# A trunk layer with mixing steps taken one group later and the merges' operand loads in another order

## The chip, the cores and the metric

The kernel runs on one core of a Trainium2 chip. The metric is the device time of one execution in microseconds (us). A core has TensorE (PE; its weight loads are listed as PEld), VectorE (DVE), ScalarE (ACT), GpSimd (POOL) and SyncE (SP). Every transfer of this kernel that the profile lists is issued from SP's queue. Each engine takes its own list of instructions in a fixed order; an instruction whose inputs or buffers aren't ready holds up all that stand behind it on that engine.

## The reference: what is computed

One layer of a decoder trunk for 1024 tokens and 16 leading meta tokens, 2048 wide, in float32. The layer normalizes the rows, makes one wide input projection, and runs two branches on it: stick-breaking attention and causal pooling over four window lengths. Each branch is gated, projected up to 2048 columns, gated again and summed; an output projection, a residual sum and a final normalization follow. The parts that matter here:

```python
zin = h @ w_in
q, k, v, g_attn, u, g_pool, m_attn, m_pool = jnp.split(zin, cuts, axis=-1)
o_attn = stick_breaking_attention(q, k, v) * silu(g_attn)
y_attn = o_attn @ w_attn_up
pooled = multiscale_pool(u)          # per group g: mean over the last 2, 4, 8 or 16 tokens, minus the token
mixed = einsum('blgc,gcd->blgd', pooled, pool_w)      # four groups of 256 channels
o_pool = mixed * pool_scale * silu(g_pool)
y_pool = o_pool @ w_pool_up
merged = sigmoid(m_attn) * y_attn + sigmoid(m_pool) * y_pool
return x + merged @ w_out
```

## The kernel before

All products are made in three parts: an operand is split into an upper part (a copy rounded to the matmul's format, ScalarE, line 116) and a lower part (the difference, VectorE or GpSimd, line 117), and `mm3` (line 137) adds upper x upper, upper x lower and lower x upper in PSUM. So each loaded tile of 128 x 512 costs one transfer of 256 KB, one ScalarE copy and one subtraction before TensorE can use it.

The input projection is done for pairs of 128-column blocks, called duos, with seven products for a two by two block matrix. A first stage makes four of them per duo and leaves partial sums in device memory (`d_nu`, `d_up`, `d_c`). A second stage, `duo_steps` (line 584), makes the three others per duo in three passes `m5`, `n4`, `p3`: each pass loads its weights in two quarters (`wr`), splits them (`wh`, `wl`), multiplies, and VectorE evicts the accumulators together with a partial sum (lines 592 and 594). The third pass goes on in the accumulators of the first.

The stages in the profiled execution: the first stage of the projection, whose last partial sums are stored at 977 us; three duos of the gates of the pooling branch (`gp`) and then, up to about 1169 us, the four pooling groups; attention, with the remaining duos between its steps, to 1876 us; the merges, from 1907 to 2270 us; the output projection to the end.

*A pooling group* (lines 675 to 714) before the change is, in program order: load and split the group's 256 x 256 mixing weights (`pwh`, `pwl`, one buffer each); load the first quarter of its `u`; run the duo, which fills `us[0]` and `us[1]`; for each of the two halves of channels build window sums by doubling (line 692: one addition for window 2, four for window 16), then the mean minus the token (line 697), then split it into `ph` and `pl`; then the mixing step: four accumulators of 128 x 512, six matmuls each, evicted by VectorE with the scale and the gate (line 713) into one of two buffers `st` and stored to `d_op`. In the last group the duo of the last gate stands between the split and the mixing step.

*The merges* (from line 897) multiply the gated branch outputs by `w_pool_up` (blocks of kind "p") and `w_attn_up` (kind "a"). One block makes 128 output columns for both halves of the tokens, `t` = 0 and 1, 24 matmuls each, and takes two weight tiles. The operands stay on chip: `op[t]` from `d_op` and `oa[t]` from `d_oa`, eight tiles for each half. `fill` (line 899) loads one of them through one of six buffers `ol` and splits it. The table `order` (line 926) begins with three "p" blocks, 0, 8 and 1, and then takes "a" blocks between. Before the loop come the two gate tiles of the first block and `op[0]` and `op[1]`; the first block's weights are issued after the sixth load of `op[0]` (`issue_after`, line 910; the `[5]` in line 906); `oa[0]` and `oa[1]` are filled ahead of the first and second block. Between the blocks GpSimd makes linear forms of blocks of `w_out` (`w_forms`, line 183), with four loads `cw` and four stores `d_wf` per round.

The building framework turns this program into one list per engine, and in doing so may move instructions that don't depend on each other. The rows of these lists are shown with the change.

Of the kernel before, what the change touches and what calls it, by code (L numbers as in the profile page):

```python
# [9 lines left out]
F32 = mybir.dt.float32  # L10
# [62 lines left out]
def trunk_kernel(  # L73
# [154 lines left out]
    with ExitStack() as actx:  # L228
# [408 lines left out]
        with ExitStack() as a0ctx:  # L637
# [36 lines left out]

            for g, win in enumerate(WINDOWS):
                pwh = a0.tile([P, 512], F32R, tag="pwh", name=nm("pwh"), bufs=1)
                pwl = a0.tile([P, 512], F32R, tag="pwl", name=nm("pwl"), bufs=1)
                load_split(pwh, pwl, pool_w[g].rearrange("(c p) d -> p c d", p=P))
                pwh, pwl = (t.rearrange("p (c d) -> p c d", d=256) for t in (pwh, pwl))
# [4 lines left out]
                duo(d, lambda key: half_of(us[key[0]], key[1], META), lambda key, t: None, us[1][:, :META])  # L684
                ph, pl = [None] * 2, [None] * 2
# [14 lines left out]
                if g == GROUPS - 1:  # L700
                    sils.append(sil_tiles())
                    silu_duo(a0, named["gp", g], sils[g])
                sil = sils[g]
                for dc in range(2):
                    dd = slice(dc * P, (dc + 1) * P)
                    ch = 2 * g + dc
                    for i in range(2):
                        t = slice(i * 512, (i + 1) * 512)
                        a = acc_tile()
                        for n, cc in enumerate((1, 0)):  # L710
                            mm3(a, pwh[:, cc, dd], pwl[:, cc, dd], ph[cc][:, t], pl[cc][:, t], n == 0, n == 1)
                        st = a0.tile([P, 512], F32, tag="st", name=nm("st"), bufs=2)
                        nc.vector.scalar_tensor_tensor(out=st, in0=a, scalar=psc[:, ch : ch + 1], in1=sil[dc][:, t], op0=ALU.mult, op1=ALU.mult)
                        nc.sync.dma_start(d_op[ch][:, t], st)
# [182 lines left out]
    with tc.tile_pool(name="pm", bufs=2, side="right", reuse_waits="tile") as pm:  # L897

        def fill(A, j, src):
            raw = pm.tile([P, 512], F32, tag="ol", name=nm("ol"), bufs=6)  # L900
            ins = nc.sync.dma_start(raw, src)
            put(A, j, raw)
            return ins
# [48 lines left out]
        for n, (kind, c) in enumerate(order):  # L952
            if n in (0, 1):
                fill_up(oa[n], d_oa, n)
# [231 lines left out]
```

## Time and profile before

| | |
|---|---|
| median of 3 runs | 2588.54 us (2584.05 to 2588.91) |
| the profiled execution's own time | 2589.82 us |
| its span, first to last instruction | 2588.1 us |
| mean granted clock of TensorE | 0.982 |
| busy share: PE, DVE, ACT, POOL | 95%, 49%, 35%, 39% |
| transfers | 457.81 MB, mean 177 GB/s |

The profile is one execution. Its page gives busy times by engine, the span in 40 slices, and the groups of instructions; the other views (waits, timelines by engine, stretches of time) are answers from the same trace. In a row such as `L713 ... st<-acc,psc,sl` the number is the line of the kernel, and out<-in are the program's names. What stands in brackets at the end of a timeline row is the idle time of the engine before the instruction and what ended it. A matmul's stated duration overlaps its neighbours; the distance from start to start is what it costs.

### The profile page before, as it was taken

The page shows a single profiled execution, that of the slowest core. Times are in us where ns is not written, and L with a number is a line of the kernel's source. Part 1 is how long each engine was busy: PE and PEld are TensorE (multiplying, and loading weights), DVE is VectorE, ACT ScalarE, POOL GpSimd, SP SyncE. Part 2 cuts the span into 40 slices and gives each one's busy share as a digit, 9 for nine tenths or more (in the row PEclk, how much of TensorE's full clock was granted, in tenths as well). Part 3 has the DMA queues.
Part 4 walks back from the last instruction along what each step waited for, and adds up shares of the span by engine and source line. Part 5 has one row for each costly group of instructions (what it writes and reads, how often), then busy time and mean ns, then how long its engine had stood idle before and what let it go on. Part 6 is the DMA issues. An engine that isn't in the chain of part 4 may idle for free.

```text
span 2588.1 us, 35874 instructions
## 1 busy us (share of the span) xinstructions
PE 2462.5 (95%) x12680; PEld 2087.6 (81%) x12680; DVE 1268.1 (49%) x2089; ACT 896.8 (35%) x1845; POOL 1005.4 (39%) x898
## 2 busy tenths in 40 slices
PE   6899999999999999899999999999949999989998
PEld 5676778888888887888888888888748888867887
DVE  5442234553333344575676567656652322445556
ACT  6421122222222234224454455545431111144243
POOL 1655555554454544233323333333104545520212
PEclk8999999999999999999999999999979999999999
DMA  5566555665555557435334443443286777675534
GB/s 181 168 208 212 196 195 201 215 232 175 179 184 183 184 179 231 133 115 151 123 118 136 127 126 117 141 126 91 86 280 208 250 237 246 225 248 183 190 124 171
DMA packets 390516, 457.81 MB, mean 177 GB/s; under 512 B 32432, under 2 KB 234544, under 8 KB 389296
## 3 DMA queue, kind: packets, MB, share of 16 engines
q1 hardware_dynamic: 390336, 455.53, 54.7%
q8 instruction: 99, 1.62, 0.3%
q14 instruction: 81, 0.66, 0.1%
HBM read 313.11 MB, written 142.31 MB: 176 GB/s over the span
## 4 chain that ended last, share of the span: by engine, by line
PE 77%; DMA 7%; DVE 6%; POOL 3%; ACT 2%; issue 2%; SPq 0%; DVEq 0%; POOLq 0%; ACTq 0%
PE acc L138 17%; PE acc L140 17%; PE acc L139 17%; PE accb L138 4%; PE accb L139 4%; PE accb L140 4%; POOL r L270 3%; PE accb L1012 2%; PE accb L1011 2%; PE accb L1010 2%; DMA mr<-d_f 2%; DMA raw<-in_w_in_dram 2%; PE tr L764 1%; DVE s L692 1%; DVE x L117 1%
## 5 line engine op out<-in xcount | busy, mean ns | idle before, releaser
L138 PE MATMUL acc<-x,wh 128*128 128x512 f32 (+2 forms) x2736 | 980.1, 359 | 25.2 <-ACT wh L116 16.4
L140 PE MATMUL acc<-x,wl 128*128 128x512 f32 (+2 forms) x2736 | 971.1, 355 | 7.3 <-DVE wl L117 6.0
L139 PE MATMUL acc<-x,wh 128*128 128x512 f32 (+2 forms) x2736 | 968.8, 354 | 0.0
L138 PEld LDWEIGHTS acc<-x,wh 128*128 128x128 f32 x2736 | 519.4, 190 | 97.0 <-ACT wh L116 22.1
L140 PEld LDWEIGHTS acc<-x,wl 128*128 128x128 f32 x2736 | 518.3, 189 | 85.3 <-DVE wl L117 13.3
L139 PEld LDWEIGHTS acc<-x,wh 128*128 128x128 f32 x2736 | 519.4, 190 | 62.7
L116 ACT ACTIVATE wh<-wr 128x512 fp32r<-128x512 f32 x408 | 256.6, 630 | 593.7 <-PE accb L139 235.4
L117 DVE TENSOR_TENSOR wl<-wr,wh 128x512 fp32r<-128x512 f32 x288 | 221.1, 770 | 248.2 <-ACT wh L116 230.0
L117 DVE TENSOR_TENSOR wl<-r,wh 128x512 fp32r<-128x512 f32 x160 | 149.5, 938 | 345.6 <-ACT wh L116 328.5
L117 POOL TENSOR_TENSOR wl<-wr,wh 128x512 fp32r<-128x512 f32 x120 | 166.6, 1388 | 346.0 <-ACT wh L116 289.3
L116 ACT ACTIVATE wh<-r 128x512 fp32r<-128x512 f32 x160 | 100.3, 631 | 474.9 <-POOL r L270 369.6
L270 POOL TENSOR_TENSOR r<-raw,raw 128x512 f32<-128x512 f32 x80 | 111.1, 1388 | 379.2 <-DMA raw<-in_w_in_dram 348.9
L138 PE MATMUL accb<-x,wh 128*128 128x512 f32 x512 | 200.2, 391 | 32.4 <-ACT wh L116 32.4
L270 POOL TENSOR_TENSOR r<-r,raw 128x512 f32<-128x512 f32 x160 | 221.6, 1385 | 12.5 <-DMA raw<-in_w_in_dram 2.5
L139 PE MATMUL accb<-x,wh 128*128 128x512 f32 x512 | 199.9, 390 | 0.0
L140 PE MATMUL accb<-x,wl 128*128 128x512 f32 x512 | 199.7, 390 | 0.0
L1010 PE MATMUL accb<-wh,x 128*128 128x512 f32 x416 | 163.8, 394 | 7.1 <-ACT wh L116 7.0
L1012 PE MATMUL accb<-wl,x 128*128 128x512 f32 x416 | 164.2, 395 | 0.2
L1011 PE MATMUL accb<-wh,x 128*128 128x512 f32 x416 | 162.7, 391 | 0.0
L748 DVE TENSOR_TENSOR_SCAN wt<-wt 128x272 f32<-128x272 f32 (+5 forms) x128 | 107.7, 842 | 110.2 <-POOL wt L743 64.8
L117 DVE TENSOR_TENSOR wl<-raw,wh 128x512 fp32r<-128x512 f32 x136 | 102.6, 765 | 100.9 <-ACT wh L116 100.8
L116 ACT ACTIVATE wh<-raw 128x512 fp32r<-128x512 f32 x160 | 97.6, 624 | 135.2 <-PE acc L139 100.3
(176 smaller groups left out, 3059.5 us busy)
## 6 DMA issues: line engine op xcount, KB each, us to landing
raw<-in_w_in_dram SPq DMA_DIRECT2D x96, 512.0 KB, 5.8
d_r<-r SPq DMA_DIRECT2D x160, 256.0 KB, 2.0
wr<-d_r SPq DMA_DIRECT2D x160, 256.0 KB, 2.9
raw<-in_w_in_dram SPq DMA_DIRECT2D x152, 256.0 KB, 5.3
wr<-in_w_in_dram SPq DMA_DIRECT2D x80, 256.0 KB, 3.0
cw<-in_w_out_dram SPq DMA_DIRECT2D x64, 256.0 KB, 5.1
d_wf<-cw SPq DMA_DIRECT2D x64, 256.0 KB, 2.8
wr<-d_wf SPq DMA_DIRECT2D x64, 256.0 KB, 3.0
```

Source lines behind the costliest of these rows:

```text
L116: nc.scalar.activation(hi, src, AF.Copy)
L117: (eng or nc.vector).tensor_tensor(out=lo, in0=src, in1=hi.bitcast(F32), op=ALU.subtract)
L138: nc.tensor.matmul(ps, wh, rh, start=first, stop=False, skip_group_check=skip)
L139: nc.tensor.matmul(ps, wh, rl, start=False, stop=False, skip_group_check=skip)
L140: nc.tensor.matmul(ps, wl, rh, start=False, stop=last, skip_group_check=skip)
L270: nc.gpsimd.tensor_tensor(out=t, in0=a, in1=b, op=ALU.add)
L692: nc.vector.tensor_tensor(out=nxt[:, lo:], in0=cur[:, lo:], in1=cur[:, lo - sh : TOK - sh], op=ALU.add)
L748: nc.vector.tensor_tensor_scan(out=rev, data0=rev, data1=rev, initial=wt[:, w : w + 1], op0=ALU.mult, op1=ALU.bypass)
L764: nc.tensor.transpose(tr[:, n, :], bt[:, off : off + P], ident)
L1010: nc.tensor.matmul(a, sh, wh, start=first and j == 0, stop=False, skip_group_check=not first)
L1011: nc.tensor.matmul(a, sl, wh, start=False, stop=False, skip_group_check=not first)
L1012: nc.tensor.matmul(a, sh, wl, start=False, stop=j == KH - 1, skip_group_check=not first)
```

## The change

Two parts. In the pooling groups the mixing step of group g is put behind the duo of group g + 1; its weights (now `pw0`, `pw1`, loaded by `mix_weights`) are loaded ahead of that duo. The last group's mixing step stays behind the last gate duo. Within a mixing step the order of the matmuls is unchanged in the program: half 1 first, half 0 second, for each accumulator.

In the merges the six buffers `ol` move to a pool of their own, `po`, opened ahead of `pm`. Program order becomes: `op[0]`; the gates of block 0; its weights, issued after the first load of `op[0]` at the earliest (`[0]`); then, between the two halves of block 0, `op[1]`; then `oa[0]` ahead of the second block and `oa[1]` ahead of the third.

```diff
@@ -672,16 +672,37 @@
                 for calls in every:
                     calls[i]()
 
+            mixed = {}
+
+            def mix_weights(g):
+                pw = [a0.tile([P, 512], F32R, tag=f"pw{m}", name=nm("pw"), bufs=1) for m in range(2)]
+                load_split(*pw, pool_w[g].rearrange("(c p) d -> p c d", p=P))
+                return [t.rearrange("p (c d) -> p c d", d=256) for t in pw]
+
+            def mix(g, pwh, pwl):
+                ph, pl = mixed.pop(g)
+                for dc in range(2):
+                    dd = slice(dc * P, (dc + 1) * P)
+                    ch = 2 * g + dc
+                    for i in range(2):
+                        t = slice(i * 512, (i + 1) * 512)
+                        a = acc_tile()
+                        for n, cc in enumerate((1, 0)):
+                            mm3(a, pwh[:, cc, dd], pwl[:, cc, dd], ph[cc][:, t], pl[cc][:, t], n == 0, n == 1)
+                        st = a0.tile([P, 512], F32, tag="st", name=nm("st"), bufs=2)
+                        nc.vector.scalar_tensor_tensor(out=st, in0=a, scalar=psc[:, ch : ch + 1], in1=sils[g][dc][:, t], op0=ALU.mult, op1=ALU.mult)
+                        nc.sync.dma_start(d_op[ch][:, t], st)
+
             for g, win in enumerate(WINDOWS):
-                pwh = a0.tile([P, 512], F32R, tag="pwh", name=nm("pwh"), bufs=1)
-                pwl = a0.tile([P, 512], F32R, tag="pwl", name=nm("pwl"), bufs=1)
-                load_split(pwh, pwl, pool_w[g].rearrange("(c p) d -> p c d", p=P))
-                pwh, pwl = (t.rearrange("p (c d) -> p c d", d=256) for t in (pwh, pwl))
+                if g:
+                    pw = mix_weights(g - 1)
                 d = named["u", g]
                 us = [tok_tile(a0, "u", F32) for _ in range(2)]
                 nc.sync.dma_start(us[0][:, META : META + HALF], d_c[d.n])
                 nc.sync.dma_start(us[0][:, :META], d_cm[d.n])
                 duo(d, lambda key: half_of(us[key[0]], key[1], META), lambda key, t: None, us[1][:, :META])
+                if g:
+                    mix(g - 1, *pw)
                 ph, pl = [None] * 2, [None] * 2
                 for cc in (1, 0):
                     u = us[cc]
@@ -697,21 +718,11 @@
                     nc.vector.scalar_tensor_tensor(out=raw, in0=cur[:, META:], scalar=1.0 / win, in1=u[:, META:], op0=ALU.mult, op1=ALU.subtract)
                     split(pool_h, pool_l, raw)
                     ph[cc], pl[cc] = pool_h, pool_l
-                if g == GROUPS - 1:
-                    sils.append(sil_tiles())
-                    silu_duo(a0, named["gp", g], sils[g])
-                sil = sils[g]
-                for dc in range(2):
-                    dd = slice(dc * P, (dc + 1) * P)
-                    ch = 2 * g + dc
-                    for i in range(2):
-                        t = slice(i * 512, (i + 1) * 512)
-                        a = acc_tile()
-                        for n, cc in enumerate((1, 0)):
-                            mm3(a, pwh[:, cc, dd], pwl[:, cc, dd], ph[cc][:, t], pl[cc][:, t], n == 0, n == 1)
-                        st = a0.tile([P, 512], F32, tag="st", name=nm("st"), bufs=2)
-                        nc.vector.scalar_tensor_tensor(out=st, in0=a, scalar=psc[:, ch : ch + 1], in1=sil[dc][:, t], op0=ALU.mult, op1=ALU.mult)
-                        nc.sync.dma_start(d_op[ch][:, t], st)
+                mixed[g] = ph, pl
+            pw = mix_weights(GROUPS - 1)
+            sils.append(sil_tiles())
+            silu_duo(a0, named["gp", GROUPS - 1], sils[-1])
+            mix(GROUPS - 1, *pw)
 
         with tc.tile_pool(name="a1", bufs=1, side="right", reuse_waits="tile") as a1:
             MK = 64 + META
@@ -894,16 +905,18 @@
         q, jj = divmod(j, QD)
         split(A[q][0][:, jj], A[q][1][:, jj], src)
 
-    with tc.tile_pool(name="pm", bufs=2, side="right", reuse_waits="tile") as pm:
+    with ExitStack() as mctx:
+        po = mctx.enter_context(tc.tile_pool(name="po", bufs=6, side="right", reuse_waits="tile"))
+        pm = mctx.enter_context(tc.tile_pool(name="pm", bufs=2, side="right", reuse_waits="tile"))
 
         def fill(A, j, src):
-            raw = pm.tile([P, 512], F32, tag="ol", name=nm("ol"), bufs=6)
+            raw = po.tile([P, 512], F32, tag="ol", name=nm("ol"))
             ins = nc.sync.dma_start(raw, src)
             put(A, j, raw)
             return ins
 
         def fill_up(A, d_o, t):
-            return [fill(A, j, d_o[j][:, t * HALF : (t + 1) * HALF]) for j in range(KH)][5]
+            return [fill(A, j, d_o[j][:, t * HALF : (t + 1) * HALF]) for j in range(KH)][0]
 
         def up_mm(w, o, c, behind):
 
@@ -927,9 +940,13 @@
         for n, k in enumerate((("p", 0), ("p", KH), ("p", 1))):
             order.remove(k)
             order.insert(n, k)
-        first = [gate("sp", 6, d_sp, 0, t) for t in range(2)]
-        op, oa = [xquads(0, HALF, xo), xquads(1, HALF, xo)], [xquads(2, HALF), xquads(3, HALF, xc)]
-        behind = [fill_up(op[t], d_op, t) for t in range(2)][0]
+        op, oa = [], []
+
+        def more(into, d_o, t, *where):
+            into.append(xquads(*where))
+            return fill_up(into[t], d_o, t)
+
+        behind = more(op, d_op, 0, 0, HALF, xo)
         sps, ms = {}, {}
 
         def sums(j):
@@ -950,12 +967,14 @@
 
         forms = w_forms(pm)
         for n, (kind, c) in enumerate(order):
-            if n in (0, 1):
-                fill_up(oa[n], d_oa, n)
+            if n in (1, 2):
+                more(oa, d_oa, n - 1, *((2, HALF), (3, HALF, xc))[n - 1])
             if kind == "p":
-                gs = [gate("sp", 6, d_sp, c, t) for t in range(2)] if n else first
+                gs = [gate("sp", 6, d_sp, c, t) for t in range(2)]
                 for t, a in up_mm(w_pu, op, c, None if n else behind):
                     nc.vector.tensor_tensor(out=gs[t], in0=a, in1=gs[t], op=ALU.mult)
+                    if n + t == 0:
+                        more(op, d_op, 1, 1, HALF, xo)
                 sps[c] = gs
             else:
                 gs = [gate("sa", 6, d_sa, c, t) for t in range(2)]
```

What the lists of the engines become at three places. First SP at the start of the merges. Before (`sp` are gate tiles, `ol` operand loads, `wr` weights, `cw` blocks of `w_out`):

```order
L923 DMA sp_18844<-d_sp_104 128x512
L901 DMA ol_18862<-d_op_80 128x512
...
L901 DMA ol_18922<-d_op_87 128x512
L901 DMA ol_18926<-d_oa_72 128x512
...
L901 DMA ol_18954<-d_oa_79 128x512
L124 DMA wr_18960<-in_w_pool_up_dram 128x4x128
L124 DMA wr_18966<-in_w_pool_up_dram 128x4x128
L189 DMA cw_19022<-in_w_out_dram 128x512
```

Between the rows shown are 14 further loads from `d_op` and six from `d_oa`: 24 operand loads stand ahead of the first weights. With the change:

```order
L850 DMA d_sp_118<-st_18766 128x512
L914 DMA ol_18849<-d_op_80 128x512
...
L914 DMA ol_18877<-d_op_87 128x512
L936 DMA sp_18881<-d_sp_104 128x512
L936 DMA sp_18883<-d_sp_104 128x512
L124 DMA wr_18887<-in_w_pool_up_dram 128x4x128
L124 DMA wr_18893<-in_w_pool_up_dram 128x4x128
L914 DMA ol_18927<-d_op_80 128x512
...
L914 DMA ol_18955<-d_op_87 128x512
L189 DMA cw_18985<-in_w_out_dram 128x512
```

Eight operand loads stand ahead of the first weights. Behind the last row come three more `cw`, the eight loads of `oa[0]`, two gates, and then the weights of the second block; behind these four stores `d_wf`, the eight loads of `oa[1]`, two gates and the weights of the third block.

Second, VectorE in the first merge block, with the change (`x<-ol` is the lower part of an operand, `sp<-accb` the eviction of one half of a block):

```order
L117 TENSOR_TENSOR x_3646_18926<-ol_18955,x_3645_18925 128x512
L975 TENSOR_TENSOR sp_18881<-accb_18897,sp_18881 128x512
L117 TENSOR_TENSOR x_3661_18994<-ol_18997,x_3660_18993 128x512
L117 TENSOR_TENSOR x_3661_18994<-ol_19001,x_3660_18993 128x512
L117 TENSOR_TENSOR x_3661_18994<-ol_19005,x_3660_18993 128x512
L975 TENSOR_TENSOR sp_18883<-accb_18959,sp_18883 128x512
L117 TENSOR_TENSOR x_3661_18994<-ol_19009,x_3660_18993 128x512
```

Before, 28 operand parts and the two weight parts stood ahead of the first eviction; now the lower parts of `oa[0]` stand behind the eviction of the first half, and those from the fourth on behind that of the second.

Third, VectorE around the mixing step of group 1 before (`s` are window sums, `st<-acc` the mixing evictions):

```order
L697 SCALAR_TENSOR_TENSOR s_9671<-s_9671,u_9459 128x1024
L117 TENSOR_TENSOR pl_9673<-s_9671,ph_9674 128x1024
L713 SCALAR_TENSOR_TENSOR st_9685<-acc_9678,psc,sl_8660 128x512
L713 SCALAR_TENSOR_TENSOR st_9695<-acc_9688,psc,sl_8660 128x512
L117 TENSOR_TENSOR pwl_9719<-wr_9720,pwh_9718 128x512
```

and, with the change, around the mixing step of group 0, which now stands at this place:

```order
L592 TENSOR_TENSOR u_9413<-nu_9419,acc_9422 128x256
L713 TENSOR_TENSOR s_9663<-u_9413 128x1039
L693 SCALAR_TENSOR_TENSOR st_9621<-acc_9614,psc,sl_8658 128x512
L693 SCALAR_TENSOR_TENSOR st_9631<-acc_9624,psc,sl_8658 128x512
L693 SCALAR_TENSOR_TENSOR st_9641<-acc_9634,psc,sl_8659 128x512
L117 TENSOR_TENSOR pl_9658<-s_9656,ph_9659 128x1024
L693 SCALAR_TENSOR_TENSOR st_9651<-acc_9644,psc,sl_8659 128x512
L713 TENSOR_TENSOR s_9665<-s_9663 128x1037
L117 TENSOR_TENSOR pw_9673<-wr_9674,pw_9672 128x512
```

The mixing evictions stood behind the chain of their own group; they now stand among the window sums of the next.

## The prediction

> **What bounds the kernel now.** I read the page first, then the waits of TensorE, then the two stages that the change touches, engine by engine.
>
> ```profile
> PE 2462.5 (95%) x12680; PEld 2087.6 (81%) x12680; DVE 1268.1 (49%) x2089; ACT 896.8 (35%) x1845; POOL 1005.4 (39%) x898
> PEclk8999999999999999999999999999979999999999
> ```
>
> TensorE is busy for 95% of the span; only stages in which it stands still, or runs at a lower granted clock, can give time. One slice of the clock row falls to 7, at about 1880 us, the start of the merges. The waits around it, and those of TensorE alone from 1000 to 1180 us (the pooling groups):
>
> ```profile
> PE accb L138 <- ACT wh L116: 32.4, 2, 31.1
> ...
> PE acc L138 <- ACT ph L116: 11.1, 5, 3.7
> PE acc L138 <- ACT wh L116: 1.9, 1, 1.9
> PE acc L139 <- DVE pl L117: 1.5, 3, 0.7
> ```
>
> One wait of 31.1 us opens the merges; eight waits of up to 3.7 us, for the split halves ph and pl of the pooled channels, stand before the mixing steps. A stretch of each kind in the windows view (columns: stretch, length, busy time of PE, PEld, DVE, ACT, POOL, granted clock, DMA share, GB/s):
>
> ```profile
> 1061.20:1064.60 3.40, 3.40 (x24) 3.17 (x23) 2.52 (x5) 0.63 (x1) 0.00 (x0) 0.94 0.42 154
> 1112.70:1116.10 3.40, 3.08 (x7) 1.97 (x8) 3.37 (x3) 0.00 (x0) 0.00 (x0) 0.52 0.74 229
> 1880.80:1907.50 26.70, 0.00 (x0) 0.00 (x0) 15.94 (x24) 15.56 (x25) 0.00 (x0) 0.50 0.92 289
> 1907.50:1911.40 3.90, 3.84 (x9) 3.02 (x10) 1.39 (x2) 0.82 (x3) 1.56 (x2) 0.50 1.03 368
> 2000.00:2100.00 100.00, 100.00 (x442) 82.78 (x442) 28.34 (x36) 11.39 (x18) 55.47 (x41) 1.00 0.71 233
> ```
>
> After each gap TensorE first runs at half clock: nine products in 3.9 us at 1907.5, where 442 in 100 us is one per 0.226 us, so a restart costs about 1.8 us more than its gap. While TensorE stands, the transfers work at 0.92 share and 289 GB/s: the wait is one for data. From 2000 us TensorE is full; what is won before passes to the end.
>
> **The mixing steps.** Each group of channels is a duo of three passes, the window sums on VectorE, and 24 mixing products. VectorE's timeline, first eviction of the first pass of each group (and of the second pass, second row), then the chain that group 2 waits for:
>
> ```profile
> 1040.45 0.42 DVE L594 TENSOR_TENSOR u<-acc,up 128x256 f32<-128x256 f32 x1 [1.27 <-PE acc L140]
> 1046.32 0.42 DVE L594 TENSOR_TENSOR u<-acc,up 128x256 f32<-128x256 f32 x1 [1.27 <-PE acc L140]
> ...
> 1068.01 0.42 DVE L594 TENSOR_TENSOR u<-acc,up 128x256 f32<-128x256 f32 x1 [1.27 <-PE acc L140]
> ...
> 1098.23 0.42 DVE L594 TENSOR_TENSOR u<-acc,up 128x256 f32<-128x256 f32 x1 [1.28 <-PE acc L140]
> ...
> 1117.46 1.23 DVE L697 SCALAR_TENSOR_TENSOR s<-s,u 128x1024 f32<-128x1024 f32 x1
> 1119.81 1.22 DVE L117 TENSOR_TENSOR pl<-s,ph 128x1024 fp32r<-128x1024 f32 x1 [1.12 <-ACT ph L116]
> ...
> 1125.69 0.75 DVE L713 SCALAR_TENSOR_TENSOR st<-acc,psc,sl 128x512 f32<-128x512 f32 x1 [0.19 <-DMA d_op<-st]
> ...
> 1129.86 0.42 DVE L594 TENSOR_TENSOR u<-acc,up 128x256 f32<-128x256 f32 x1 [1.28 <-PE acc L140]
> ```
>
> The groups take 27.56, 30.22 and 31.63 us. Their own work: a pass takes 5.87 us (1040.45 to 1046.32), the third has 256 columns for a mean of 264 and takes 5.69, the mixing 24 x 0.226 = 5.42; together 5.87 + 5.87 + 5.69 + 5.42 = 22.85 us. The excess is 4.7 + 7.4 + 8.8 = 20.9 us, and with the pl wait of 0.7 before the last mixing 21.6. That is idle time and half clock together. The excess grows with the window because one more VectorE addition (about 1.2 us) stands in each half's chain per doubling.
>
> Moved behind the next duo, a mixing step needs ph and pl some 17 us later; the chain of 5 to 10 us lies under the three passes. What VectorE has to do per group: for window 8 two halves of three additions, mean and lower part, 5 x 1.23 each, 12.3; evictions 6 x 0.42 + 0.2 = 2.7; mixing evictions 4 x 0.75 = 3.0; lower parts of weights 4 x 0.7 = 2.8: 20.8 us, under 22.85. Window 16 adds 2.5, 23.3, but its chain has mixing step 2 and the gate duo (three passes of 24 products, 16.3 us) in front of its own mixing. In VectorE's queue the mixing evictions now stand among the chain of the next group, and they wait for TensorE and for the store two before; what is behind them and urgent is the eviction of the next first pass, needed 5.87 us after it is ready, when the third pass accumulates on the same accumulator. The step's transfers move on SP's queue too:
>
> ```profile
> d_op<-st SPq DMA_DIRECT2D x16, 256.0 KB, 2.4
> ...
> wr<-in_pool_w_dram SPq DMA_DIRECT2D x4, 256.0 KB, 3.0
> ```
>
> Four stores per step, 2.4 us each from two buffers, with products every 1.36 us (6 x 0.226): the third eviction waits about 1 us, on VectorE, which has it to spare. The weights pw keep one of the four wr buffers until the mixing before is done; three are left for six weight loads in 22.85 us, each held for about 3.0 + 0.6 + 1.4 = 5 us: one per 1.7 us against one per 2.9 needed. I leave 0.35 us per step for a new first wait on an accumulator. **Gain 21.6 - 1.1 = 20.5 us**; bounds: 21.6, and about 10 if in each of three groups three chain parts of 1.2 us come to stand before what TensorE waits for.
>
> **The merges.** SP's queue before, then what ScalarE, VectorE and TensorE make of it:
>
> ```profile
> 1878.26 0.88 SPq L923 DMA_DIRECT2D sp<-d_sp  x2
> 1879.23 14.19 SPq L901 DMA_DIRECT2D ol<-d_op  x16
> 1894.01 6.69 SPq L901 DMA_DIRECT2D ol<-d_oa  x8
> 1900.75 0.97 SPq L124 DMA_DIRECT2D wr<-in_w_pool_up_dram  x2
> 1901.77 2.23 SPq L189 DMA_DIRECT2D cw<-in_w_out_dram  x4
> 1904.43 10.57 SPq L901 DMA_DIRECT2D ol<-d_oa  x8
> 1915.06 0.90 SPq L923 DMA_DIRECT2D sp<-d_sp  x2
> 1916.00 0.98 SPq L124 DMA_DIRECT2D wr<-in_w_pool_up_dram  x2
> ```
>
> ```profile
> 1884.22 3.96 ACT L116 ACTIVATE x<-ol 128x512 fp32r<-128x512 f32 x6 [6.40 <-DMA ol<-d_op]
> ...
> 1906.88 0.63 ACT L116 ACTIVATE wh<-wr 128x512 fp32r<-128x512 f32 x1 [0.21 <-DMA wr<-in_w_pool_up_dram]
> ...
> 1921.22 0.63 ACT L116 ACTIVATE wh<-wr 128x512 fp32r<-128x512 f32 x1 [2.89 <-DMA wr<-in_w_pool_up_dram]
> ```
>
> ```profile
> 1884.88 4.05 DVE L117 TENSOR_TENSOR x<-ol,x 128x512 fp32r<-128x512 f32 x6 [7.72 <-ACT x L116]
> ...
> 1938.59 0.69 DVE L958 TENSOR_TENSOR sp<-accb,sp 128x512 f32<-128x512 f32 x1 [2.27 <-PE accb L140]
> 1944.03 0.69 DVE L958 TENSOR_TENSOR sp<-accb,sp 128x512 f32<-128x512 f32 x1 [1.59 <-PE accb L140]
> ```
>
> ```profile
> 1907.56 0.80 PE L138 MATMUL accb<-x,wh 128*128 128x512 f32 x1 [31.13 <-ACT wh L116]
> 1921.90 0.50 PE L138 MATMUL accb<-x,wh 128*128 128x512 f32 x1 [1.32 <-ACT wh L116]
> ```
>
> Before, the first weights are issued behind 24 operand loads. Now they stand behind eight. Step by step:
>
> Start. The first load goes out at 1878.26, 0.97 us earlier and with two gate loads less before it (256 KB at 289 GB/s is 0.91 us each). Its lower part was ready at 1884.88 + 0.69; now about 1884. Loads 7 and 8 need the first two of the six buffers, so they go at 1884.1 and 1884.8, the gates and weights by 1886.1. The weights took 1900.75 to 1906.88, 6.1 us, in an equally full queue: 1892.2, and TensorE starts 0.68 later, at **1892.9 instead of 1907.56, 14.7 us earlier**. Bounds: 5.2 us of landing (1916.00 to 1921.22) gives 1892.0; two more transfers in front, 1894.7.
>
> Block 0 takes 12.8 us as before (1907.56 to about 1920.4, half clock included), to 1905.7. Its second half starts at 1900.3; those eight loads are issued from 1887 to 1895 and split by 1901, one per 0.7 us: enough.
>
> Block 1 is where the stall goes. Its weights are transfers 35 and 36 in SP's order, behind 24 operand loads, four of the w_out blocks, and gates. From 1880.8, where the stretch at 289 GB/s begins, at 0.91 us each number 35 lands at 1912.5; at 368 GB/s, 0.71 each, at 1905.7. By the queues: the seventh attention load needs the buffer of the first, whose lower part stands on VectorE behind the eviction of block 0's first half, ready at 1900.5; so the weights go out near 1906.5 and take 5.2 us: 1911.7. The two agree. TensorE starts block 1 at 1912.4, idle for 6.7 us where it was 1.3 before, and restarts cold, 1.8. It ends at 1912.4 + 10.9 + 1.8 = 1925.1.
>
> Block 2's weights stand behind the w_out stores and the other eight attention loads, of which the seventh again waits for a lower part; they go out near 1918.5 and land by 1924.6: no wait, or one of 1 us. Block 2 ends at 1936.0; before, its last eviction began at 1944.03, 0.2 after its product. **Gain 8 us.** Upper bound, no stall between blocks: 1892.9 + 12.8 + 21.8 = 1927.5, gain 16. Lower bound: start 1.8 later (1894.7), 3.6 more at block 1 (four transfers that go out beside its weights, 0.91 each), 0.9 at block 2 (6.1 us of landing for 5.2) and a cold restart there, 1.8; together 8.1: gain about 0.
>
> The pool of its own moves addresses only; the first load stays behind the last gate store, which ends at 1878, so by itself it is worth nothing here, and no wait is removed by it.
>
> Sum against the profiled execution's own time, 2589.82 us (span 2588.1 plus 1.7): 2589.8 - 20.5 - 8 = 2561.3. That execution lies 1.3 us above the median of 2588.54, which the result is held against; I take **2560.5**, and give the rivals as differences from it.
>
> [...]
>
> [...]
>
> **The rivals.** *The queue keeps up.* If the transfers run at 368 GB/s, block 1's weights land by 1905.7 and a wait of 1 us is left: 7 of the 8.5 us lost at block 1 come back, **2553.5**. For it: the 1.03 share at 1907.5. Against: 289 over the 26.7 us with just these loads, and the six buffers, which hold SP back.
>
> *The stall only moves.* The gap taken from block 0 comes back at blocks 1 and 2 (the lower bound above): 8 us less gain, **2568.5**. For it: SP is one queue, and the same transfers must pass before the attention blocks.
>
> *The mixing half works*: its lower bound, 10.5 us less gain, **2571**. Against: VectorE has room by the count above.
>
> *Slower.* VectorE's queue makes the duos wait: the mixing evictions wait for stores, the chain parts behind them shift, and the first-pass eviction comes x us late. TensorE loses x - 5.9 at each of three mixings and the gate duo. To eat 28 us, 4(x - 5.9) must exceed it: x over 13. At x = 15 the time is 2560.5 + 36.4 = **2597**. For it: the mixing evictions are queued ahead of chain parts on an in-order engine. Against: the 20.8 us of work in 22.85.
>
> *The change does nothing*: excluded, since TensorE's and SP's orders differ as shown.
>
> **Chances.** Forecast 0.55 (own range 2556 to 2566), queue keeps up 0.15, stall only moves 0.14, mixing half 0.08, no change 0.03, slower 0.05. About 0.2%, 5 us, is what a measurement here can tell from no change: faster 0.92, same 0.03, slower 0.05. The range takes the forecast and the first three rivals: 2551 to 2572.
>
> **What would show it.** Right: first eviction to first eviction near 23 us in the three groups; no wait on ph or pl; first merge product at 1893 less the 20 us won before, so near 1872; one wait of 5 to 8 us, ended by ScalarE's wh, before block 1; full afterwards. Wrong: periods above 25 us; waits of TensorE on evictions in the groups; a gap before block 0 above 20 us; gaps at blocks 2 and 3; idle time elsewhere that answers the gain.

## The result and the profile after

The changed kernel takes **2563.71 us** (median of 4 runs, 2560.89 to 2566.15) against 2588.72 for the kernel before on the same chip (4 runs): a ratio of **0.9903, 95% interval 0.9883 to 0.9924**, 25 us less. The prediction was 2560.5 us (own range of the forecast 2556 to 2566). The profiled execution of the change took 2566.15 us, the longest of its four, with a span of 2564.4, which is 23.7 us less than the span of 2588.1 profiled before.

The page of the changed kernel, busy time and granted clock:

```profile
PE 2456.4 (96%) x12680; PEld 2087.2 (81%) x12680; DVE 1269.7 (50%) x2089; ACT 897.4 (35%) x1845; POOL 1008.3 (39%) x898
PEclk9999999999999999999999999999979999999999
```

The number of instructions is the same as before; the slice of the merges still shows a clock of 7. The gain has to be read stage by stage. TensorE's waits with the change, first in the pooling groups (1000 to 1180 us), then in the merges (1840 to 1990 us):

```profile
PE acc L138 <- ACT wh L116: 3.6, 1, 3.6
PE acc L140 <- DVE wl L117: 1.3, 1, 1.3
PE acc L138 <- DVE u L592: 0.3, 1, 0.3
PE acc L138 <- DVE st L693: 0.2, 1, 0.2
...
PE accb L138 <- ACT wh L116: 25.9, 2, 16.0
```

The eight waits for ph and pl (11.1 and 1.5 us before) are gone. The 3.6 us for wh lie at 1015 us, ahead of the groups, where the kernel before had 1.9. In the merges the total fell only from 32.4 to 25.9 us: a wait of 31.1 and one of 1.3 became one of 16.0 and one of 10.0. VectorE's timeline of the groups with the change, the first eviction of each group (L594) and two rows of mixing evictions (L693), the second of them the last:

```profile
1039.83 0.43 DVE L594 TENSOR_TENSOR u<-acc,up 128x256 f32<-128x256 f32 x1 [1.26 <-PE acc L140]
...
1058.39 0.75 DVE L594 TENSOR_TENSOR u<-acc,up 128x256 f32<-128x256 f32 x2
...
1081.49 0.41 DVE L594 TENSOR_TENSOR u<-acc,up 128x256 f32<-128x256 f32 x1
...
1099.68 0.75 DVE L693 SCALAR_TENSOR_TENSOR st<-acc,psc,sl 128x512 f32<-128x512 f32 x1 [2.56 <-DMA d_op<-st]
...
1108.48 0.76 DVE L594 TENSOR_TENSOR u<-acc,up 128x256 f32<-128x256 f32 x2
...
1148.68 1.41 DVE L693 SCALAR_TENSOR_TENSOR st<-acc,psc,sl 128x512 f32<-128x512 f32 x2 [3.58 <-DMA d_op<-st]
```

From the first eviction to the start of that last row it is 1148.68 - 1039.83 = 108.9 us; before, the same stretch ran from 1040.45 to the last L713 row:

```profile
1167.99 1.41 DVE L713 SCALAR_TENSOR_TENSOR st<-acc,psc,sl 128x512 f32<-128x512 f32 x2 [3.14 <-DMA d_op<-st]
```

127.5 us, so the mixing steps give **18.7 us**. What TensorE makes of the stretch, in the windows view (columns as in the prediction), before and then with the change:

```profile
1040.40:1168.00 127.60, 114.81 (x728) 103.00 (x727) 86.50 (x99) 31.14 (x49) 32.62 (x20) 0.95 0.41 124
```

```profile
1039.80:1148.70 108.90, 107.11 (x731) 99.52 (x731) 84.51 (x99) 31.03 (x49) 32.15 (x20) 1.00 0.46 146
```

12.8 us of idle time became 1.8, and the clock went from 0.95 to 1.00; the busy time itself fell by 7.7 us for the same products, and I put that down to the lower clock after the old gaps. Before, TensorE came to the mixing products of group 2 after 2.47 us of idle time, and the stretch from there, 1112.70:1116.10 in the prediction, has a clock of 0.52:

```profile
1112.66 1.95 PE L138 MATMUL acc<-ph,pwh 128*128 128x512 f32 x4 [2.47 <-ACT ph L116]
```

The prediction put half clock behind each gap; after the 0.72 us that TensorE stood before 1080.68, the stretch shows 1.00:

```profile
1080.68 1.20 PE L138 MATMUL acc<-ph,pwh 128*128 128x512 f32 x4 [0.72 <-ACT ph L116]
```

```profile
1080.60:1084.00 3.40, 3.20 (x12) 2.10 (x12) 3.40 (x3) 0.55 (x2) 1.85 (x1) 1.00 0.76 224
```

The merges, first products of blocks 0 and 1 on TensorE, and the evictions of the first three blocks on VectorE (first and last row):

```profile
1872.80 0.79 PE L138 MATMUL accb<-x,wh 128*128 128x512 f32 x1 [15.96 <-ACT wh L116]
1896.09 0.80 PE L138 MATMUL accb<-x,wh 128*128 128x512 f32 x1 [9.98 <-ACT wh L116]
```

```profile
1880.70 0.69 DVE L975 TENSOR_TENSOR sp<-accb,sp 128x512 f32<-128x512 f32 x1
...
1920.63 0.69 DVE L975 TENSOR_TENSOR sp<-accb,sp 128x512 f32<-128x512 f32 x1 [1.17 <-PE accb L140]
```

Attention ended (the first product's start less its wait) at 1872.80 - 15.96 = 1856.8 us against 1876.4 before, 19.6 earlier. Block 2's last eviction is at 1920.63 against 1944.03, 23.4 earlier. So the merges added **3.8 us**, not the 8 predicted.

### The profile page after: what moved, and what is told of

It reads as the page before. It is cut to its first block, busy times and chain, and to the rows that moved or that the text cites. A ratio compares the mean times of both kernels' runs of the same rounds, so it can differ in the third digit from the quotient of the medians.

```text
span 2564.4 us, 35884 instructions
## 1 busy us (share of the span) xinstructions
PE 2456.4 (96%) x12680; PEld 2087.2 (81%) x12680; DVE 1269.7 (50%) x2089; ACT 897.4 (35%) x1845; POOL 1008.3 (39%) x898
## 4 chain that ended last, share of the span: by engine, by line
PE 79%; DMA 6%; DVE 4%; POOL 3%; ACT 1%; issue 1%; SPq 0%; DVEq 0%; POOLq 0%; ACTq 0%
PE acc L138 17%; PE acc L140 17%; PE acc L139 17%; PE accb L138 4%; PE accb L140 4%; PE accb L139 4%; PE accb L1031 3%; PE accb L1029 3%; PE accb L1030 3%; POOL r L270 3%; DMA raw<-in_w_in_dram 2%; DMA mr<-d_f 2%; PE tr L775 1%; DVE wl L117 1%; DVE bt L760 1%
## 5 line engine op out<-in xcount | busy, mean ns | idle before, releaser
L140 PEld LDWEIGHTS acc<-x,wl 128*128 128x128 f32 x2736 | 519.2, 190 | 83.5 <-DVE wl L117 11.4
L117 DVE TENSOR_TENSOR wl<-wr,wh 128x512 fp32r<-128x512 f32 x288 | 220.8, 769 | 241.7 <-ACT wh L116 227.1
L117 DVE TENSOR_TENSOR wl<-r,wh 128x512 fp32r<-128x512 f32 x160 | 148.6, 932 | 329.2 <-ACT wh L116 322.6
L117 POOL TENSOR_TENSOR wl<-wr,wh 128x512 fp32r<-128x512 f32 x120 | 166.3, 1386 | 337.9 <-ACT wh L116 294.6
L138 PE MATMUL accb<-x,wh 128*128 128x512 f32 x512 | 201.6, 394 | 25.9 <-ACT wh L116 25.9
L1029 PE MATMUL accb<-wh,x 128*128 128x512 f32 x416 | 163.7, 393 | 6.2 <-ACT wh L116 6.0
L117 DVE TENSOR_TENSOR wl<-raw,wh 128x512 fp32r<-128x512 f32 x136 | 105.3, 782 | 113.4 <-ACT wh L116 113.4
```

The source lines that it names most:

```text
L117: (eng or nc.vector).tensor_tensor(out=lo, in0=src, in1=hi.bitcast(F32), op=ALU.subtract)
L138: nc.tensor.matmul(ps, wh, rh, start=first, stop=False, skip_group_check=skip)
L140: nc.tensor.matmul(ps, wl, rh, start=False, stop=last, skip_group_check=skip)
L1029: nc.tensor.matmul(a, sh, wh, start=first and j == 0, stop=False, skip_group_check=not first)
```

## Experiments

Ten kernels were run, in three groups, each group on one chip and beside the kernel before on that chip. Its medians there were 2588.80, 2585.55 and 2585.72 us, so kernels of different groups are compared by their ratio to it. Waits of TensorE are those of the profiled execution; waits under 1 us are left out.

| kernel | median us | ratio to before, 95% | wait before block 0, block 1 (us) |
|---|---|---|---|
| the change | 2563.71 | 0.9903, 0.9883 to 0.9924 | 16.0, 10.0 |
| mixing alone | 2568.58 | 0.9921, 0.9896 to 0.9946 | 30.4, 2.2 |
| merges alone | 2584.41 | 0.9986, 0.9972 to 1.0000 | 15.5, 11.1 |
| weights ahead | 2560.04 | 0.9882, 0.9862 to 0.9902 | 14.0, 2.4, then 3.4 and 2.5 |
| weights first | 2543.91 | 0.9820, 0.9801 to 0.9839 | 8.7, none |
| change, no hold | 2547.07 | 0.9858, 0.9829 to 0.9887 | 8.5, none, then 2.0 (block 4) |
| mixing, no hold | 2546.71 | 0.9847, 0.9827 to 0.9867 | 9.8, none, then 1.2 (block 4) |
| w_out sums later | 2574.82 | 0.9949, 0.9931 to 0.9967 | 15.8, 4.7 |
| one more addition | 2566.54 | 0.9919, 0.9900 to 0.9938 | 17.1, 10.0 |
| eight buffers | 2560.00 | 0.9899, 0.9879 to 0.9918 | 14.2, 4.1 |
| no pool of its own | 2566.36 | 0.9926, 0.9903 to 0.9948 | 16.3, 8.8 |

### Each half of the change alone

The first kernel takes the part of the diff around the mixing steps (lines 675 to 725 of the change), the second the part of the merges.

> The kernel before with the shifted mixing steps alone; the merges stay as they were. Theory (the two parts of the change are independent): the groups of pass 1 give what the change gave up to attention's last product, 19 to 20 us, so about 2569.5 us; the merges keep a first wait of about 31 us and a second of about 1.3 us. Rival (the mixing steps are worth their sum of 20.5 us and the merges of the change gave less because something shifted into them): 2568 us or less, with the attention ending 20.5 us earlier. Rival (the mixing steps only help together with the new loads): above 2575 us.

> The kernel before with the new order of the merges' loads alone; the mixing steps stay where they were. Theory (independent parts): 3.8 us less than before, about 2585 us, with a wait of about 16 us before the first block, and one of about 10 us before the second. Rival (the second wait is 10 us instead of 6.7 because of the mixing part): 8 us less than before, 2580.5 us, with a second wait near 6.7 us. Rival (the stall only moves): 2588 to 2589 us.

The parts add up: 0.9921 x 0.9986 = 0.9907 against 0.9903 together. The mixing alone gives 20 us, the merges alone 4 us (whose interval reaches no gain). TensorE's waits in the merges of the second kernel, whose mixing steps are the old ones:

```profile
PE accb L138 <- ACT wh L116: 26.6, 2, 15.5
```

15.5 and 11.1 us: the second wait came out longer than the predicted 6.7 by the merges' own doing, and the rival that puts it on the mixing part falls.

### Weights ahead of the attention loads

```diff
         for n, (kind, c) in enumerate(order):
+            ops = weights(w_pu if kind == "p" else w_au, c, None if n else behind)
             if n in (1, 2):
                 more(oa, d_oa, n - 1, *((2, HALF), (3, HALF, xc))[n - 1])
...
-                for t, a in up_mm(w_pu, op, c, None if n else behind):
+                for t, a in up_mm(ops, op):
```

(`weights` is the first half of `up_mm`, made a function of its own; lines left out are marked `...`.)

> The changed kernel, with the weights of each block of the merges issued ahead of the attention operand's loads of the same place (blocks 1 and 2). Theory (the 10 us before block 1 are the place of its weights in the queue): the wait before block 1 falls below 1 us, blocks 0 to 2 run without a gap, and the time is 8 to 10 us below the changed kernel's, 2554 to 2556 us. Rival (the transfers as a whole are late, the weights are only the last of them): the wait comes back before block 3, which needs the 16 loads of the attention operand, at 6 us or more: 2560 to 2563 us. Rival (ScalarE, not the queue, is late with the weights, since it works through the splits in order): the wait stays at 8 us or more.

The 10 us before block 1 fell to 2.4, but the theory's price did not come: two new waits stand before blocks 2 and 3. The same view of TensorE from 1903 us:

```profile
1905.05 0.50 PE L138 MATMUL accb<-x,wh 128*128 128x512 f32 x1 [3.42 <-ACT wh L116]
1920.34 0.50 PE L138 MATMUL accb<-x,wh 128*128 128x512 f32 x1 [2.51 <-ACT wh L116]
```

SP's queue in this kernel shows why:

```profile
1882.46 0.98 SPq L124 DMA_DIRECT2D wr<-in_w_pool_up_dram  x2
1883.55 11.91 SPq L914 DMA_DIRECT2D ol<-d_oa  x8
...
1899.28 1.63 SPq L124 DMA_DIRECT2D wr<-in_w_pool_up_dram  x2
```

Block 2's weights stand behind eight attention loads that take 11.9 us to issue. The waits for weights sum to 22.3 us instead of 25.9. The place further ahead in the same queue moved 5.9 us of the wait (3.4 and 2.5) to the next blocks' weights. The rival "the transfers as a whole are late" gives the same time (2560.04 us lies in its range), and the next run tells it apart.

### Weights out of the queue

The fourth kernel also puts the first weights ahead of the first operand half, with no hold:

```diff
-        behind = more(op, d_op, 0, 0, HALF, xo)
+        ops0 = weights(w_pu, order[0][1])
+        more(op, d_op, 0, 0, HALF, xo)
...
+            ops = weights(w_pu if kind == "p" else w_au, c) if n else ops0
```

> As the run before it, and the first block's weights are asked for ahead of the first token half too, without being held back, so that they can be loaded while attention still runs. Theory (the 16 us before block 0 are 8 loads of an operand and then the weights, one after the other): the weights are there first, TensorE starts on the first of the 8 splits and the wait falls to 6 to 9 us; the rest of block 0 follows the loads at their rate, so that 3 to 6 us of it come back inside the block: 2549 to 2553 us. Rival (the last split of the 8, not the weights, sets the start and the end of block 0): at most 2 us below the run before it. Rival (the early weights push out loads that the last attention steps need): attention ends later, 2556 us or more.

It is below the range of its own theory, 20 us under the change. The weight loads that find a free `wr` buffer now go out while attention runs, down to the two of block 3 (`in_w_attn_up`, issued at 1854.21 us). The wait left is the one for the first operand part, 8.7 us, with 0.7 us for another part inside block 0 and 0.3 us for weights later. If the transfers as a whole had been late, the attention operand would have held block 3; it did not.

Both kernels, before and after, share one constraint that had kept the weights back: the first of them may be issued only after an operand load (`tc.issue_after` in `up_mm`), and the later ones followed it. The fifth and sixth kernels drop that constraint alone, once in the change and once in the kernel with the mixing steps shifted and the merges' loads in the old order (all 16 `op` loads, then attention):

```diff
-                for t, a in up_mm(w_pu, op, c, None if n else behind):
+                for t, a in up_mm(w_pu, op, c, None):
```

> The changed kernel with one line undone that both kernels have: the first block's weights are no longer held back until the first operand load is out; the order of the loads in the program is that of the change. Theory (what the merges wait for is weights in one queue behind operand loads, and the hold is what put all of them there): all four wr buffers are filled while attention still runs, the waits on ScalarE's wh before blocks 0 and 1 go, one wait of 8 to 9 us for the first operand part is left, and the time is that of the run with the weights first, 2543 to 2546 us. Rival (that run needed the weights written ahead of the loads in the program as well): waits on wh of 5 us or more stay, 2550 to 2558 us.

> The shifted mixing steps alone, with the merges as before (16 operand loads, then the attention loads), but with the first weights not held back. Theory (the order of the operand loads is worth nothing once the weights are out of the queue, since the first token half comes first in both): 2543 to 2547 us, one wait of 8 to 9 us before block 0, and at most 2 us between the blocks. Rival (the weights between the token halves are what gives the gain of the merges): 2552 us or more, with a first wait of 15 us or more.

SP's queue, and TensorE's first product of the merges, in the change without the hold:

```profile
1847.26 3.25 SPq L124 DMA_DIRECT2D wr<-in_w_pool_up_dram  x2
1852.75 3.20 SPq L124 DMA_DIRECT2D wr<-in_w_attn_up_dram  x2
1856.55 7.86 SPq L914 DMA_DIRECT2D ol<-d_op  x8
```

```profile
1862.70 0.80 PE L138 MATMUL accb<-x,wh 128*128 128x512 f32 x1 [8.48 <-ACT x L116]
```

and the waits of TensorE in the merges of the sixth kernel:

```profile
PE accb L138 <- ACT x L116: 9.8, 1, 9.8
PE accb L138 <- ACT wh L116: 1.2, 1, 1.2
```

The wait for wh before block 0 is gone in both; what is left for weights is 2.0 and 1.2 us before block 4. The fifth kernel came out 1 us above the range of its theory, the sixth inside it. Their ratios, 0.9858 and 0.9847, are not told apart, so the new order of the loads, worth some 4 us in the profiled executions while the weights are held, showed no worth once they are not. The fourth kernel's median lies 3 us lower, but its interval overlaps theirs; whether its place for the weights adds anything stays open. The fourth and the sixth lie below both kernels of the case by their intervals; that of the fifth just touches the change's.

### What made the wait before block 1 ten microseconds

Two kernels take one suspect each from the change. The first starts the sums of w_out three blocks later:

```diff
-            for _ in range(2 if n % 2 else 1):
+            for _ in range((2 if n % 2 else 1) if n > 2 else 0):
                 next(forms, None)
```

> The changed kernel with the sums of w_out (four loads, four GpSimd subtractions, four stores each) started after the first three blocks of the merges instead of beside them. Theory (the wait before block 1 came out at 10 us and not at 6.7 because the four loads stand in the queue ahead, 0.9 us each, and because GpSimd's subtractions slowed VectorE's lower parts from 0.7 to 1.46 us): the wait falls to 6 to 7 us, the lower parts of the attention operand take 0.7 us each, 2559 to 2561 us. Rival (only the queue's length matters): the wait falls by 3.6 us, but the lower parts stay at 1.4 us. Rival (the six buffers hold SP, whatever stands between): the wait stays at 9 us or more, 2563 us.

The wait fell by 5.3 us, to 4.7, more than expected. VectorE's lower parts (`x<-ol,x`) in the same place (grouped rows: busy us, mean ns), with the change from 1885.5 to 1890.3, while GpSimd subtracts, and then in this kernel from 1881.5 to 1885.5, while it does not:

```profile
L117 DVE TENSOR_TENSOR x<-ol,x 128x512 fp32r<-128x512 f32 x3 | 4.4, 1512 | 4.5 <-ACT x L116 4.5
```

```profile
L117 DVE TENSOR_TENSOR x<-ol,x 128x512 fp32r<-128x512 f32 x6 | 3.7, 686 | 0.0
```

1.51 against 0.69 us each. Both halves of the theory are seen, but they don't weigh the same. The first of the two rows also says that VectorE stood idle for 4.5 us before these parts: the operand had not come yet. SP's first attention loads and the weights of block 1, and ScalarE's first parts of that operand, with the change and then in this kernel:

```profile
1877.99 10.93 SPq L914 DMA_DIRECT2D ol<-d_oa  x8
1889.91 0.98 SPq L124 DMA_DIRECT2D wr<-in_w_pool_up_dram  x2
1885.20 3.87 ACT L116 ACTIVATE x<-ol 128x512 fp32r<-128x512 f32 x6 [5.29 <-DMA ol<-d_oa]
```

```profile
1876.56 6.71 SPq L914 DMA_DIRECT2D ol<-d_oa  x8
1884.27 0.98 SPq L124 DMA_DIRECT2D wr<-in_w_pool_up_dram  x2
1880.26 1.24 ACT L116 ACTIVATE x<-ol 128x512 fp32r<-128x512 f32 x2 [0.39 <-DMA ol<-d_oa]
```

With the four w_out loads ahead, the first attention load reaches ScalarE 7.2 us after its issue, without them 3.7. VectorE's first lower part, which frees the buffer for the seventh load, starts at 1885.86 against 1881.64 us, 4.2 us later; of the 5.6 us by which the weights go out later, some 1.4 are left for the slower lower parts. This split is read off two traces; no run slows the one without the other. The total is 11 us worse than the change, where 3 to 5 us less were expected: the sums pile up later, and between 2200 and 2300 us the first products of the final stage (L1029) wait longer, with the change and then with the sums later:

```profile
PE accb L1029 <- ACT wh L116: 6.0, 2, 5.4
```

```profile
PE accb L1029 <- ACT wh L116: 14.7, 5, 5.1
```

The second kernel gives the operand loads two more buffers:

```diff
-        po = mctx.enter_context(tc.tile_pool(name="po", bufs=6, side="right", reuse_waits="tile"))
+        po = mctx.enter_context(tc.tile_pool(name="po", bufs=8, side="right", reuse_waits="tile"))
...
-                r = pm.tile([P, HALF], F32, tag="r", name=nm("r"), bufs=4)
+                r = pm.tile([P, HALF], F32, tag="r", name=nm("r"), bufs=2)
```

> The changed kernel with eight buffers for the operand loads instead of six (the room comes from the buffers r of the later sums, two instead of four, which nothing uses before the fourth block). Theory (the six buffers, freed by VectorE's lower parts, hold SP back and with it the weights: SP waited 10.8 us for VectorE's x in this stretch): the first weights go out 1 to 2 us earlier, and the wait before block 1 falls from 10.0 to 6 to 8 us; 2559 to 2562 us. Rival (the transfers' own rate is the limit, SP only waits where they would queue anyway): the waits stay at 15 to 16 and 9 to 10 us, within 2 us of the changed kernel's time.

SP's waits in the change between 1857 and 1910 us have this at the top:

```profile
SPq L914 <- DVE x L117: 10.8, 14, 1.7
```

With eight buffers that wait is 0.4 us. The first eight loads on SP, six buffers and then eight, and the waits of TensorE in the merges with eight:

```profile
1858.66 7.14 SPq L914 DMA_DIRECT2D ol<-d_op  x8
```

```profile
1858.71 3.99 SPq L914 DMA_DIRECT2D ol<-d_op  x8
```

```profile
PE accb L138 <- ACT wh L116: 18.3, 2, 14.2
```

They go out in 4.0 us instead of 7.1, and 4.1 us of waiting is left before block 1. The windows view from the first load to the weights of block 1, six buffers and then eight, shows what they did to the rate of the transfers (the last number, GB/s):

```profile
1858.60:1889.90 31.30, 13.31 (x48) 10.45 (x48) 16.90 (x22) 15.21 (x25) 5.77 (x4) 0.73 0.85 270
```

```profile
1858.70:1881.30 22.60, 10.18 (x39) 8.28 (x40) 13.33 (x20) 12.51 (x20) 2.52 (x2) 0.70 1.01 343
```

The same list of transfers is issued in 22.6 us instead of 31.3. So the buffers hold SP, and what the prediction took for the rate of the transfers was in part the rate at which the buffers came free. The time moves less than the waits: the profiled span is 7.5 us below the change's, but the ratio of 0.9899 is not told apart from 0.9903. The profiled executions exaggerate here, as they are the shortest of four with eight buffers and the longest of four with six. Whether the halved `r` buffers take anything is open.

### The pool, and the room on VectorE

> The changed kernel with the operand buffers in the merges' common pool, as before, instead of a pool of their own. Theory (the first load stands behind the last gate store in SP's queue either way): first merge product and both waits (16.0 and 10.0 us) as in the changed kernel within 1 us, the time within 3 us of it. Rival (the pool of its own lets the loads out before the rest of the old pool's memory is free): the first load goes out 1 us or more later, and the first wait is 17 us or more.

```diff
-        po = mctx.enter_context(tc.tile_pool(name="po", bufs=6, side="right", reuse_waits="tile"))
...
-            raw = po.tile([P, 512], F32, tag="ol", name=nm("ol"))
+            raw = pm.tile([P, 512], F32, tag="ol", name=nm("ol"), bufs=6)
```

Waits of 16.3 and 8.8 us, a ratio whose interval overlaps the change's, and the first load 1.8 us after attention's last product in both: the pool of its own shows no effect.

> The changed kernel with one more window addition on VectorE for each half of a group (1.24 to 1.6 us each, 8 in all, the result of which is not used; two per group). In the kernel before such an addition was worth 0.7 to 1.35 us of a group's period each, since the excess of the periods grew from 4.7 to 7.4 to 8.8 us with two more of them. Theory (the chain now lies under the next duo's passes, and VectorE was busy for 84.5 of 108.9 us there): at most 1 us more than the changed kernel in the groups, first eviction to last mixing eviction 108.9 to 110 us. Rival (VectorE is the bound of the groups now, its order more than its load): 5 to 12 us more, with waits of TensorE on evictions.

```diff
+                    nxt = tok_tile(a0, "s", F32)
+                    nc.vector.tensor_tensor(out=nxt[:, 1:], in0=u[:, 1:], in1=u[:, : TOK - 1], op=ALU.add)
                     cur, lo, sh = u, 0, 1
```

The groups in the windows view of this kernel:

```profile
1041.80:1151.80 110.00, 107.56 (x728) 99.10 (x727) 95.95 (x107) 30.64 (x49) 36.12 (x20) 1.00 0.46 145
```

VectorE's busy time rose from 84.5 to 96.0 us, the stretch from 108.9 to 109.9 (1041.85 to 1151.76). Where two more additions had added 2.7 and 1.4 us to a group's period before (from 4.7 to 7.4 to 8.8), eight of them, 11.4 us of VectorE's work, now added 1.1. TensorE waited there for one eviction (1.4 us) and one lower part (0.8 us); the median, 2566.54 us, has a ratio that is not told apart from the change's. The rival by which VectorE had become the bound, 5 to 12 us more, falls.

## Why the prediction was right, and where its sizes were off

**The mixing steps: right, 18.7 us for 20.5.** The waits for ph and pl went, and the half clock with them (0.95 to 1.00 over the stretch), as the sum had it; the kernel with this part alone gave 20 us by its runs. The missing 1.8 us are two small terms. What could be won was 12.8 + 7.7 = 20.5 us by the windows rows, where the sum had 21.6. And TensorE still stood for 1.8 us, where 1.1 had been left for new waits on an accumulator: 1.3 for one lower part of weights on VectorE (L117, wl), which was not in the sum, and 0.3 and 0.2 for accumulators (L592, L693). 20.5 - 1.8 = 18.7. The sign to look for, "first eviction to first eviction near 23 us", was badly chosen: the periods are 18.6, 23.1 and 27.0 us. The first has no mixing step in it any more. In the third the eviction comes late, because VectorE's mixing evictions waited for their stores (2.56 us at 1099.68), while TensorE did not stand (27.00 us busy of the 27.00 from 1081.50 on): it needs the accumulator only one pass later. The mean of the three is 22.9.

**The start of the merges: right.** Predicted 16.5 us of idle time and the first product near 1872; measured 15.96 and 1872.80.

**Block 1: right in kind, 10.0 us for 6.7.** This is the step that failed in size: "the weights go out near 1906.5", 13.6 us after TensorE's start in block 0. They went out at 1889.91, 17.1 us after it, and were split from 1895.40 on, 5.5 us later, where 5.2 was assumed. The 3.5 us are in the first attention loads. The prediction let the seventh of them wait for a buffer that VectorE frees behind the eviction of block 0's first half. That eviction began at 1880.70, 7.9 us after the start where 7.6 was forecast; but the first lower part began only at 1885.86, since the first attention load, with the four w_out loads ahead of it, had not landed, and the three parts then took 1.51 us each under GpSimd's subtractions. So the limit was the buffers, as predicted, but what kept them was a late load more than VectorE's order. Taking the w_out sums away shortened the wait by 5.3 us, two more buffers by 5.9; together that is 11.2 us of a wait of 10.0, so the two gains overlap, as either lets SP through. That the prediction's two estimates agreed was no confirmation, as they had one cause: the 289 GB/s by which I counted the transfers had been measured under the same six buffers.

**The sum of the merges.** Predicted gain 8; start 0.5 better, block 0 13.3 us instead of 12.8, the wait 3.3 more, block 1 13.5 instead of 12.7: 8 + 0.5 - 0.5 - 3.3 - 0.8 = 3.9, against 3.8 measured. Block 2 had no wait, as predicted. (The 12.8 was itself read a little short: by the row of the second product it was 1921.90 - 1.32 - 1907.56 = 13.0 us before.)

**The whole.** 18.7 in the groups, 3.8 in the merges, 0.6 before the first group, and 0.6 in the passes and blocks elsewhere: 23.7 us of the profiled span, where the sum had 28.5. Of the 4.8 us that are missing, 4.2 are in the merges, most of them the wait before block 1, which ate half of their gain, and 1.8 in the groups; the 1.2 us won elsewhere were not forecast, and that they made up for some of it is luck. So the mechanisms were right and the size of one term was not. The 3 us between 2560.5 and the median of 2563.71 are no more than the runs of one kernel differ by (2560.89 to 2566.15), so they are not put down to one term. The sum itself, 28.5 off the median of 2588.54, gives 2560.0; the 2560.5 that was taken is half a microsecond above it.

**The rivals.** "The queue keeps up" did not come: the stretch ran at 270 GB/s and not at 368, and even with eight buffers and 343 GB/s a wait of 4.1 us was left where it had 1 us. "The stall only moves" was half true: of 15.2 us won before block 0, the wait before block 1 took 8.7 (10.0 where the prediction's row had 1.3). The slower case, VectorE's order, did not come, and the added additions show that VectorE had room.

One of the stretches shown went above the 368 GB/s of the first rival, but a short one, the start of block 1 with the change:

```profile
1896.10:1899.00 2.90, 2.90 (x7) 2.28 (x8) 1.35 (x2) 0.63 (x1) 0.00 (x0) 0.50 1.04 391
```

It ran at 391 GB/s for 2.9 us.

## What to carry to other kernels

Where a wait for weights opens a stage, ask first what holds back their issue: here one ordering constraint, taken from two kernels, was worth some 12 us in one (the intervals just touch) and 19 us in the other by the ratios (0.9903 to 0.9858, 0.9921 to 0.9847), and without it the new order of the loads showed no effect. A rate of transfers read off a stage in which the queue waits for buffers may be the rate at which buffers come free; here it rose from 270 to 343 GB/s with two more buffers. A dependent chain moved under the next piece of work cost next to nothing here (1.1 us for 11.4 us of added additions), as its engine still had slack; adding work to it shows that more surely than the busy share does.

## What the runs showed of the hardware

VectorE's two-operand lower parts on 128x512 took 1.51 us each with the change (three from 1885.86 on, 4.38 us), while GpSimd subtracted four blocks of the same size (from 1883.69 on, 6.00 us). With the sums of w_out later, when GpSimd was idle there, they took 0.69 us each. So beside GpSimd's subtractions each part took 0.82 us longer; what makes it so, no run here shows.
